# The last down products of a two-layer encoder: halves in another order, an output that already holds its bias, one token tile written transposed

## The chip, the cores and the metric

The kernel runs on one core of one Trainium2 chip. The metric is the device time of one execution in microseconds (us). Before the change, three timed runs gave 1536.09, 1539.66 and 1539.62 us, so the median is 1539.62 us.

## The reference

The program is an encoder trunk of two layers over one sequence of 512 tokens with 1024 channels, all in float32. Each layer has an attention mixer with gated branches, a layer norm, a squared-ReLU MLP with a gated per-layer embedding, and a second layer norm. The change touches the very start (the first input projection) and the very end, which computes the last lines of this (shortened):

```
for i in range(DEPTH):                       # DEPTH = 2
    h = mixer(x)                             # starts with x @ w_in
    x = layer_norm(ALPHA * x + h, ln1_g[i], ln1_b[i])
    mlp = square(relu(x @ w_up[i])) @ w_down[i]
    gate = sigmoid(x @ w_ple_gate[i] + b_ple_gate[i])
    ple = gate * (p[i] @ w_ple[i])
    x = layer_norm(ALPHA * x + mlp + ple, ln2_g[i], ln2_b[i])

layer_norm(x, g, b) = (x - mean) * rsqrt(var + 1e-5) * g + b     # over the 1024 channels of a token
```

## The kernel before

**Precision.** Every large product is made of three TensorE products in the type fp32r: each operand is split into a high part and a low remainder, and high·high, high·low and low·high are summed in PSUM. ScalarE makes the high part by a cast, VectorE the low part by a subtraction (`split`, lines 228 and 229).

**The start.** The residual x comes transposed, as eight tiles `xs` of 128 channels by 512 tokens (line 343), through a pool of four buffers, so that the fifth load waits until the first tile has been split. The weights come in sets of 128 x 1024 (`fetch`, line 249, issued on the queue of SyncE; `prep` splits them). `weights` (called with a look-ahead of two sets) fetches and splits the sets that come next. Only set 0 is asked for between the loads of x, right after the first of them; it comes in three cuts. Sets 1 and 2 are asked for when the first product starts, in program order behind all eight loads of x. The first projection, `linear_k_outer` with the name "start", takes sets 0 to 3, of which set j holds the channels of x tiles 2j and 2j+1. Four output tiles of 128 x 512 are summed side by side, so each set gives 24 products. Here the order of the engines' instructions is set by a planner, which simulates a timeline.

**The MLP.** The hidden layer of 4096 is made in four quarters (`q`). Each quarter's contribution to the output is a product of a 512 x 1024 hidden block with a 1024 x 1024 block of `w_down`, made by seven products of half blocks instead of eight (class `Down`; sums and differences of weight blocks by `add`, of hidden blocks by `hidden`). The seven are in the tuple `PRODUCTS`. Product n has two halves s = 0 and 1, each of which makes a 128 x 512 block in 12 matmuls; below, 4/0 is the half s = 0 of product 4. The output is four token tiles y[0] to y[3] of 128 x 1024. `gather` adds or subtracts a half to its place in y by one VectorE instruction (line 1037). For s = 0 these are y[0] upper columns for product 4, y[2] upper for product 5, y[2] lower for product 6. For s = 1 they are y[1] and y[3] in the same way. Product 3 goes to three places of y (`spread`, line 1028). Products 5 and 6 use one PSUM bank per half: 6 is summed on top of 5, after 5 has been gathered.

**The second norm.** Class `Tokens` computes it: `moments` (line 861) takes the moments of 512 columns, and `statistics` aggregates them (line 868), negates the mean, adds epsilon, takes the reciprocal, lets ScalarE take the root (line 873), subtracts the mean from the whole tile on ScalarE (line 875), and refines the root on VectorE (lines 877 to 879). `scaled` multiplies by the root and by the row g2 (line 896). In the last layer the bias row is added by an accumulating DMA from HBM into y (`add_row`, line 924) for tiles 0 and 1, and by VectorE or GpSimd from a row in SBUF (b2r) for tiles 2 and 3.

**The order at the end.** In the last quarter the products 4, 5 and 6 run with both halves of one before the next: 4/0, 4/1, 5/0, 5/1, 6/0, 6/1. The orders of TensorE, VectorE and ScalarE there are those in which the program is written (`manual_schedule`); those of GpSimd and of the DMA queue of SyncE are the planner's. Tiles 0 and 1 have all their columns after product 4, but they share one `statistics` call. Tiles 2 and 3 each end with a half of product 6. Six DMAs write the output.

Of the kernel before, what the change touches and what calls it, by code (L numbers as in the profile page):

```python
# [10 lines left out]
F32 = mybir.dt.float32  # L11
# [3 lines left out]
ALU = mybir.AluOpType  # L15
# [5 lines left out]
P = 128  # L21
# [180 lines left out]
def build(nc, tc, plan, down, xT, xN, pT, wst, vec, rows, sink, cst, out):  # L202
# [3 lines left out]
    with ctx:  # L206
# [20 lines left out]
        def split(hi, lo, src):  # L227
            nc.scalar.copy(hi, src)  # L228
            nc.vector.tensor_tensor(lo, src, hi.bitcast(F32), ALU.subtract)  # L229
# [110 lines left out]
        with tc.tile_pool(name="xp", bufs=4) as xp:  # L340
            for k in range(KT):
                xs = xp.tile([P, S], F32, tag="xs", name=f"xs{k}")
                nc.sync.dma_start(xs, xT[:, k, :])
                if k == 0:
                    ahead(0)
                split(X[k][0], X[k][1], xs)

# [503 lines left out]
        class Tokens:  # L851
# [5 lines left out]
            def moments(self, a, h):  # L857
                if self.st is None:
                    self.st = self.pool.tile([P, 4, 2, 6], F32, tag="nst", name="nst" + self.name, bufs=1)
                    self.mv = self.pool.tile([P, 4, 2], F32, tag="nmv", name="nmv" + self.name, bufs=1)  # L860
                nc.vector.bn_stats(self.st[:, a, h], self.y[a][:, h * 512:(h + 1) * 512])

            def statistics(self, a, n=2, root=False):
# [3 lines left out]
                for i in range(a, a + n):  # L867
                    nc.vector.bn_aggr(self.mv[:, i], self.st[:, i].rearrange("p h c -> p (h c)"))
                nc.vector.tensor_scalar(m, self.mv[:, a:a + n, 0], -1.0, None, ALU.mult)
# [4 lines left out]
                for i in range(n):  # L874
                    nc.scalar.activation(self.y[a + i], self.y[a + i], AF.Identity, bias=m[:, i:i + 1])
                if root:
# [14 lines left out]
                for i in range(n):  # L891
                    self.rs[a + i] = r[:, i:i + 1]

            def scaled(self, a, g, c=slice(0, D)):
                x = self.y[a][:, c]
                nc.vector.scalar_tensor_tensor(x, x, self.rs[a], g[:, c], ALU.mult, ALU.mult)
# [30 lines left out]
        class Down:  # L927
# [76 lines left out]
            def product(self, q, n, then=None):  # L1004
                name, _, tag, first = self.PRODUCTS[n]
                hi, lo = self.op[name]
                if first:
                    self.bank = getattr(self, "bank", {})
                    self.bank[tag] = [bank(tag, f"dn{self.l}_{q}_{n}_{s}") for s in range(2)]
                ps = self.bank[tag]  # L1010
                for s in range(2):
                    tok = slice(s * P, (s + 1) * P)
                    for c in range(2):
                        w = self.sets[n, c]
                        for i in range(2):
                            k, cols = 2 * c + i, slice(i * 512, (i + 1) * 512)
                            for m, (a, b) in enumerate(((hi, 0), (hi, 1), (lo, 0))):
                                nc.tensor.matmul(ps[s], a[:, k, tok], w[b][:, cols], start=first and not (k or m),  # L1018
                                                 stop=k == 3 and m == 2, skip_group_check=True)
                    last = self.gather(q, n, s, ps[s])  # L1020
                    if then:
                        with tc.issue_after(last.ins):
                            then(s)

# [6 lines left out]
            def gather(self, q, n, s, ps):  # L1031
                y, v, lo, up = self.y, self.v[s], slice(0, 512), slice(512, D)
# [4 lines left out]
                return nc.vector.tensor_tensor(to, to, ps, ALU.subtract if n in (2, 4, 5) else ALU.add)  # L1037
# [21 lines left out]
        for l in range(DEPTH):  # L1059
            last = l == DEPTH - 1  # L1060
            vraw = cp.tile([P, 32], F32, tag="vraw", name=f"vraw{l}", bufs=2)
# [4 lines left out]
            b1, b2 = vraw[:, 16:24], vraw[:, 24:32]  # L1066
# [129 lines left out]
            with tc.manual_schedule(engines={PE}):  # L1196
                for q in range(FQ):
# [58 lines left out]
            with tc.manual_schedule(engines={PE, DVE, ACT}):  # L1256
                dn.cut(q, 6, 0)
                dn.product(q, 4, lambda s: tn.moments(s, 1))
                if last:
                    tn.statistics(0, root=True)  # L1260
                else:
                    ahead(at[0], at[0] + 2)

                def fifth(s):
                    tn.moments(2 + s, 1)
                    if last:
                        if s:
                            tn.scaled(0, g2)
                        return
                    if not s:  # L1270
                        tn.statistics(0)
                        return
                    ahead(at[0] + 1)
                    tn.scaled(0, g2)
                    tn.scaled(1, g2)

                dn.product(q, 5, fifth)
                if last:
                    half = [slice(h * 512, (h + 1) * 512) for h in range(2)]
                    nc.scalar.activation(y[1], y[1], AF.Copy, scale=tn.rs[1])  # L1280
                    for c in half:
                        nc.gpsimd.tensor_tensor(y[1][:, c], y[1][:, c], g2[:, c], ALU.mult)
# [4 lines left out]
                    def sixth(s):  # L1287
                        tn.moments(2 + s, 0)
                        tn.statistics(2 + s, 1, root=True)
                        if not s:  # L1290
                            for c in half:
                                nc.gpsimd.tensor_tensor(y[2][:, c], y[2][:, c], g2[:, c], ALU.mult)

                    dn.product(q, 6, sixth)
                    tn.scaled(3, g2, half[1])
                    nc.gpsimd.tensor_tensor(y[3][:, half[1]], y[3][:, half[1]], b2r[:, half[1]], ALU.add)
                    for c in half:
                        nc.vector.scalar_tensor_tensor(y[2][:, c], y[2][:, c], tn.rs[2], b2r[:, c], ALU.mult, ALU.add)
                        nc.sync.dma_start(out[2][:, c], y[2][:, c])
                    nc.scalar.dma_start(out[3][:, half[1]], y[3][:, half[1]])  # L1300
                    tn.scaled(3, g2, half[0])
                    nc.vector.tensor_tensor(y[3][:, half[0]], y[3][:, half[0]], b2r[:, half[0]], ALU.add)
                    nc.sync.dma_start(out[3][:, half[0]], y[3][:, half[0]])
                else:
# [61 lines left out]
```

## Time and profile before

| | |
|---|---|
| profiled execution, its own time | 1536.4 us |
| its span | 1534.6 us |
| granted TensorE clock | 0.997 |
| TensorE busy | 1512.5 us (99%) |
| VectorE busy | 1017.7 us (66%) |
| ScalarE busy | 763.7 us (50%) |
| GpSimd busy | 246.4 us (16%) |
| DMA | 189.47 MB, mean 123 GB/s |

The span is the time from the first to the last record of the execution; its own time lies 1.8 us above it. PE is TensorE, DVE VectorE, ACT ScalarE, POOL GpSimd and SP SyncE; ACTq, SPq and POOLq are the engines' issuing sides, which start DMAs. A row of the timeline gives the start in us, the duration in us, the engine, the line, the operation, what it writes and reads, and how many instructions of one kind were merged (x2). In brackets stands how long the engine had been idle and what released it.

### The profile page before, as it was taken

The numbers are of one execution on the slowest core, as the hardware profiler recorded it, in microseconds if no ns is written. First come the engines' busy times: TensorE is split into PE (matmuls) and PEld (weight loads), VectorE is DVE, ScalarE is ACT, GpSimd is POOL, SyncE is SP. The second block draws the span as 40 slices with busy tenths as digits, with TensorE's granted clock in tenths as the row PEclk, the third lists the DMA queues.
The fourth block names the chain that finished last, engine by engine and source line by source line (L and its number), as shares of the span: only waits on it lengthen the run. The fifth ranks groups of instructions, "written<-read, shape, count | busy, mean of one in ns | idle before, by whom it ended". The sixth has DMA issues, their size and how long they took to land.

```text
span 1534.6 us, 19685 instructions
## 1 busy us (share of the span) xinstructions
PE 1512.5 (99%) x7438; PEld 1243.0 (81%) x7438; DVE 1017.7 (66%) x1751; ACT 763.7 (50%) x1244; POOL 246.4 (16%) x213
## 2 busy tenths in 40 slices
PE   9999999999999999999999999999999999999996
PEld 7778888888888888888887888878888888888885
DVE  5666553558568777686876665534585776767868
ACT  5777764344344443444557776633442444444442
POOL 1212220110011120202012112111100201111022
PEclk9999999999999999999999999999999999999998
DMA  7544665345612414141355445574455233231403
GB/s 234 124 112 111 149 151 166 123 137 152 205 55 87 133 54 153 42 161 59 100 168 137 114 112 138 138 209 134 149 149 183 69 109 111 82 124 56 151 1 96
DMA packets 53951, 189.47 MB, mean 123 GB/s; under 512 B 6496, under 2 KB 6880, under 8 KB 53856
## 3 DMA queue, kind: packets, MB, share of 16 engines
q1 hardware_dynamic: 43200, 151.74, 30.0%
q0 software_dynamic: 9936, 36.18, 12.5%
q8 instruction: 58, 0.95, 0.3%
q10 hardware_dynamic: 720, 0.30, 0.1%
q14 instruction: 37, 0.30, 0.1%
HBM read 155.16 MB, written 4.19 MB: 104 GB/s over the span
## 4 chain that ended last, share of the span: by engine, by line
PE 88%; DVE 5%; DMA 3%; ACT 2%; issue 1%; POOL 0%; SPq 0%; POOLq 0%; DVEq 0%; ACTq 0%
PE dn L1018 16%; PE ps_up L281 8%; PE ps_up L280 8%; PE ps_up L282 8%; PE pg L288 2%; PE wo L288 2%; PE wo L287 2%; PE wo L286 2%; PE pg L286 2%; PE pg L287 2%; PE sa L439 1%; PE pta L417 1%; DMA raw<-wst 1%; PE sb L439 1%; PE ps_start L281 1%
## 5 line engine op out<-in xcount | busy, mean ns | idle before, releaser
L228 ACT CAST whi<-wst 128x1024 fp32r<-128x1024 f32 (+2 forms) x120 | 121.2, 1010 | 257.8 <-PE ps_up L281 115.5
L229 DVE TENSOR_TENSOR wlo<-wst,whi 128x1024 fp32r<-128x1024 f32 (+2 forms) x120 | 145.5, 1216 | 128.2 <-ACT whi L228 127.4
L280 PE MATMUL ps_up<-xhi,whi 128*128 128x512 f32 x512 | 199.2, 389 | 0.0
L281 PE MATMUL ps_up<-xlo,whi 128*128 128x512 f32 x512 | 199.2, 389 | 0.0
L282 PE MATMUL ps_up<-xhi,wlo 128*128 128x512 f32 x512 | 199.2, 389 | 0.0
L991 POOL TENSOR_TENSOR hr<-r 128x512 f32<-128x512 f32 x64 | 102.2, 1597 | 552.2 <-ACT r L983 531.7
L280 PEld LDWEIGHTS ps_up<-xhi,whi 128*128 128x128 f32 x512 | 96.1, 188 | 20.0
L282 PEld LDWEIGHTS ps_up<-xhi,wlo 128*128 128x128 f32 x512 | 96.1, 188 | 19.9
L281 PEld LDWEIGHTS ps_up<-xlo,whi 128*128 128x128 f32 x512 | 96.1, 188 | 19.9
L228 ACT CAST whi<-raw 128x1024 fp32r<-128x1024 f32 x56 | 58.0, 1053 | 97.0 <-PE ps_up L281 57.7
L228 ACT CAST dhi<-raw 128x1024 fp32r<-128x1024 f32 x56 | 58.7, 1052 | 82.2 <-PE dn L1018 60.1
L1037 DVE TENSOR_TENSOR y<-y,dn 128x512 f32<-128x512 f32 x96 | 65.0, 681 | 38.7 <-PE dn L1018 38.7
L235 POOL DMA_DIRECT2D wlo<-wst x54 | 47.4, 877 | 244.8 <-ACT wlo L234 157.6
L971 DVE TENSOR_TENSOR raw<-raw,raw 128x1024 f32<-128x1024 f32 x64 | 86.3, 1348 | 0.2
L233 ACT CAST whi<-wst 128x1024 fp32r<-128x1024 f32 x54 | 56.7, 1051 | 42.5 <-PE ps_start L281 6.9
L229 DVE TENSOR_TENSOR wlo<-raw,whi 128x1024 fp32r<-128x1024 f32 x56 | 68.1, 1219 | 14.1 <-ACT whi L228 14.1
L229 DVE TENSOR_TENSOR dlo<-raw,dhi 128x1024 fp32r<-128x1024 f32 x56 | 69.2, 1238 | 5.8 <-ACT dhi L228 5.8
L234 ACT ACTIVATE wlo<-whi 128x1024 fp32r<-128x1024 f32 x54 | 57.3, 1061 | 0.9
L288 PE MATMUL pg<-bhi,xlo 128*128 128x512 f32 x128 | 49.9, 390 | 1.2 <-DVE xlo L915 1.2
L1018 PE MATMUL dn<-whi,smh 128*128 128x512 f32 x128 | 50.1, 394 | 0.7 <-DVE y L1037 0.7
L1018 PE MATMUL dn<-wlo,smh 128*128 128x512 f32 x128 | 50.6, 395 | 0.1
L1018 PE MATMUL dn<-whi,sml 128*128 128x512 f32 x128 | 49.9, 390 | 0.0
(846 smaller groups left out, 4014.0 us busy)
## 6 DMA issues: line engine op xcount, KB each, us to landing
wst<-wst SPq DMA_DIRECT2D x187, 512.0 KB, 3.5
raw<-wst SPq DMA_DIRECT2D x64, 512.0 KB, 4.2
wlo<-wst POOLq DMA_DIRECT2D x54, 512.0 KB, 4.6
y<-rows POOLq DMA_DIRECT2D x14, 512.0 KB, 7.2
row<-rows SPq DMA_DIRECT2D x7, 512.0 KB, 8.8
wst<-wst SPq DMA_DIRECT2D x9, 256.0 KB, 2.7
xs<-xT SPq DMA_DIRECT2D x8, 256.0 KB, 6.0
y<-xN SPq DMA_DIRECT2D x4, 512.0 KB, 5.7
```

The source lines that it names most:

```text
L228: nc.scalar.copy(hi, src)
L229: nc.vector.tensor_tensor(lo, src, hi.bitcast(F32), ALU.subtract)
L280: nc.tensor.matmul(ps, w[0][:, s], x[0], start=start, stop=False, skip_group_check=part)
L281: nc.tensor.matmul(ps, w[0][:, s], x[1], start=False, stop=False, skip_group_check=part)
L282: nc.tensor.matmul(ps, w[1][:, s], x[0], start=False, stop=stop, skip_group_check=part)
L286: nc.tensor.matmul(ps, x[0], w[0][:, c], start=start, stop=False)
L287: nc.tensor.matmul(ps, x[0], w[1][:, c], start=False, stop=False)
L288: nc.tensor.matmul(ps, x[1], w[0][:, c], start=False, stop=stop)
L971: nc.vector.tensor_tensor(to, to, other, ALU.add)
L991: nc.gpsimd.tensor_tensor(h.rearrange("p s t -> p (s t)"), r, r, ALU.mult)
L1018: nc.tensor.matmul(ps[s], a[:, k, tok], w[b][:, cols], start=first and not (k or m), stop=k == 3 and m == 2, skip_group_check=True)
L1037: return nc.vector.tensor_tensor(to, to, ps, ALU.subtract if n in (2, 4, 5) else ALU.add)
```

## The change

At the start, x's pool has eight buffers, and set 1 is fetched and split right after x's tile 1. At the end of the last layer the halves run in the order 4/0, 5/0, 4/1, 6/0, and then 5/1 and 6/1 in two pieces of 256 columns each (second pieces in another PSUM bank). The cut of product 5's first weight set moves one half earlier. Each tile has its own statistics, split in two (`in_two`): the first part up to the root, the second with the refinement; between them stands the gather and the moments of another half. Tiles 0, 1 and 2 are no longer centred by themselves: ScalarE applies scale and shift in one instruction per 512 columns. Tiles 0 and 1 are multiplied by g2 on GpSimd and added by an accumulating DMA to the output in HBM, into which the bias row has been written beforehand. Tile 2 is transposed on TensorE, gets g2 and the bias per partition on ScalarE (the vectors `vec` get eight more columns for g2), and is written transposed; the host puts it back. Tile 3 gets (y - mean) * g2 on VectorE (`weighed`), the second half of it after the refinement, and then times root plus bias, in two halves with a DMA each.

```diff
-        with tc.tile_pool(name="xp", bufs=4) as xp:
+        with tc.tile_pool(name="xp", bufs=8) as xp:
...
                 split(X[k][0], X[k][1], xs)
+                if k == 1:
+                    ahead(1)
...
-            def statistics(self, a, n=2, root=False):
+            def steps(self, a, n=2, root=False, centre=True):
...
-                nc.vector.tensor_scalar(m, self.mv[:, a:a + n, 0], -1.0, None, ALU.mult)
+                if centre:
+                    nc.vector.tensor_scalar(m, self.mv[:, a:a + n, 0], -1.0, None, ALU.mult)
                 nc.vector.tensor_scalar(v, self.mv[:, a:a + n, 1], LN_EPS, None, ALU.add)
                 if root:
                     nc.vector.reciprocal(c, v)
                     nc.scalar.activation(rs, c, AF.Sqrt)
-                for i in range(n):
+                for i in range(n if centre else 0):
                     nc.scalar.activation(self.y[a + i], self.y[a + i], AF.Identity, bias=m[:, i:i + 1])
+                if centre is None:
+                    self.weighed(a, 0)
+                yield
...
+                if centre is None:
+                    self.weighed(a, 1)
+                elif not centre:
+                    nc.vector.scalar_tensor_tensor(h, self.mv[:, a:a + n, 0], -1.0, r, ALU.mult, ALU.mult)
+                    for i in range(n):
+                        for y in (self.y[a + i][:, :512], self.y[a + i][:, 512:]):
+                            nc.scalar.activation(y, y, AF.Identity, bias=h[:, i:i + 1], scale=self.rs[a + i])
...
+            def weighed(self, a, h):
+                c = slice(h * 512, (h + 1) * 512)
+                nc.vector.scalar_tensor_tensor(self.y[a][:, c], self.y[a][:, c], self.mv[:, a, 0:1], self.g[:, c],
+                                               ALU.subtract, ALU.mult)
...
+            def half(self, q, n, s, c0=0, c1=512):
...
+                if c0:
+                    self.bank[tag, s] = self.bank.get((tag, s)) or bank("mm", f"dn{self.l}_{q}_{n}_{s}_{c0}")
+                ps = (self.bank[tag, s] if c0 else self.bank[tag][s])[:, c0:c1]
...
-                                if s:
+                                if s != (last and q == FQ - 1 and n == 3):
                                     dn.cut(q, n + 2, 0)
...
+                    with tc.issue_after(dn.ready.ins):
+                        for a in range(2):
+                            nc.sync.dma_start(out[a], rows[l, 4].partition_broadcast(P))
...
+                    def taken(n, s, *cols):
+                        dn.gather(q, n, s, dn.half(q, n, s, *cols), *cols)
+
+                    def weighed(a):
+                        for c in (slice(0, 512), slice(512, D)):
+                            nc.gpsimd.tensor_tensor(y[a][:, c], y[a][:, c], g2[:, c], ALU.mult)
+                        nc.gpsimd.dma_start(out[a], y[a], accum_op=ALU.add)
...
+                    def turned_out(a, h, tag):
+                        tp = bank(tag, f"out{a}_{h}")
+                        ks = range(4 * h, 4 * h + 4)
+                        for i, k in enumerate(ks):
+                            nc.tensor.transpose(tp[:, i * P:(i + 1) * P], y[a][:, k * P:(k + 1) * P], ident)
+                        for i, k in enumerate(ks):
+                            nc.scalar.activation(z[:, k], tp[:, i * P:(i + 1) * P], AF.Identity, bias=b2[:, k:k + 1],
+                                                 scale=gc[:, k:k + 1])
+                        to = out[a].rearrange("(p k) (j t) -> p (k j) t", k=1, j=KT)
+                        nc.sync.dma_start(to[:, ks.start:ks.stop], z[:, ks.start:ks.stop])
+
+                    def roots(a):
+                        return tn.in_two(a, 1, root=True, centre=False)
+
+                    taken(4, 0)
+                    tn.moments(0, 1)
+                    rest = roots(0)
+                    taken(5, 0)
+                    tn.moments(2, 1)
+                    rest()
+                    weighed(0)
+                    taken(4, 1)
+                    tn.moments(1, 1)
+                    rest = roots(1)
+                    taken(6, 0)
+                    tn.moments(2, 0)
+                    rest()
+                    weighed(1)
+                    for n, h in ((5, 2), (6, 0)):
+                        for i in range(2):
+                            taken(n, 1, i * 256, i * 256 + 256)
+                            tn.moments(3, h + i, 4)
+                            if h + i == 2:
+                                rest = roots(2)
+                            if h + i == 3:
+                                rest()
+                    rest = tn.in_two(3, 1, root=True, centre=None)
+                    rest()
+                    for h, tag in enumerate(("pt", "o")):
+                        turned_out(2, h, tag)
+                    for h, issue in enumerate((nc.sync, nc.scalar)):
+                        c = slice(h * 512, (h + 1) * 512)
+                        nc.vector.scalar_tensor_tensor(y[3][:, c], y[3][:, c], tn.rs[3], b2r[:, c], ALU.mult, ALU.add)
+                        issue.dma_start(out[3][:, c], y[3][:, c])
...
-                    for a in range(2):
-                        add_row(y[a], l, 4)
-                        nc.sync.dma_start(out[a], y[a])
...
-                    dn.product(q, 6, sixth)
-                    tn.scaled(3, g2, half[1])
-                    nc.gpsimd.tensor_tensor(y[3][:, half[1]], y[3][:, half[1]], b2r[:, half[1]], ALU.add)
-                    for c in half:
-                        nc.vector.scalar_tensor_tensor(y[2][:, c], y[2][:, c], tn.rs[2], b2r[:, c], ALU.mult, ALU.add)
-                        nc.sync.dma_start(out[2][:, c], y[2][:, c])
-                    nc.scalar.dma_start(out[3][:, half[1]], y[3][:, half[1]])
-                    tn.scaled(3, g2, half[0])
-                    nc.vector.tensor_tensor(y[3][:, half[0]], y[3][:, half[0]], b2r[:, half[0]], ALU.add)
-                    nc.sync.dma_start(out[3][:, half[0]], y[3][:, half[0]])
```

More of the change, by code (lines that the diff above doesn't have):

```diff
@@ L1004, in product @@
             def product(self, q, n, then=None):
[L1005 to L1010, printed above, removed]
-                for s in range(2):
[L1012 to L1020, printed above, removed]
+                for s in range(2):
+                    last = self.gather(q, n, s, self.half(q, n, s))
                     if then:
@@ L1261, in build @@
+                    rest()
[5 more added lines that the diff above has]
+                        issue.dma_start(out[3][:, c], y[3][:, c])
                 else:
+                    dn.product(q, 4, lambda s: tn.moments(s, 1))
@@ L1262, in build @@
                     ahead(at[0], at[0] + 2)
[L1264 to L1277, printed above, removed]
@@ L1305, in build, with fifth @@
+                    def fifth(s):
+                        tn.moments(2 + s, 1)
+                        if not s:
+                            tn.statistics(0)
+                            return
+                        ahead(at[0] + 1)
+                        tn.scaled(0, g2)
+                        tn.scaled(1, g2)
+                    dn.product(q, 5, fifth)
                     PL = [(ph[:, k], pl[:, k]) for k in range(2)]
@@ L1364 @@
     r = run_bass_kernel_spmd(nc, [arrays], core_ids=[0])
-    return np.asarray(r.results[0]["out"]).reshape(1, S, D)
+    o = np.array(r.results[0]["out"])
+    o[2] = o[2].reshape(P, KT, P).transpose(2, 1, 0).reshape(P, D)
+    return o.reshape(1, S, D)
```

60 lines of the change are left out of this document (35 added, 25 removed).

## The prediction

> **What bounds the kernel now.** I read the page first, then the chain of waits, the stretches, and the timelines of the first 30 and the last 55 us.
>
> ```profile
> PE 88%; DVE 5%; DMA 3%; ACT 2%; issue 1%; POOL 0%; SPq 0%; POOLq 0%; DVEq 0%; ACTq 0%
> ```
>
> TensorE holds 88% of the chain, so an edit pays where PE is idle: at the first products and behind the last one. Both are what the change touches. The stretches up to the last matmul and behind it:
>
> ```profile
> 1505.00:1521.10 16.10, 16.10 (x72) 13.01 (x70) 14.60 (x29) 4.70 (x7) 4.57 (x4) 1.00 0.00 1
> 1521.10:1534.60 13.50, 0.02 (x1) 0.00 (x0) 7.82 (x17) 2.33 (x4) 4.89 (x4) 0.61 0.82 233
> ```
>
> Columns: length, then busy time and count of PE, PE's loads, DVE, ACT and POOL, the clock, the DMA share, GB/s. In the first PE is full, DVE nearly, and the DMA engines idle. Then 13.5 us run after PE's end, with DVE busy for 7.8 of them. The end in VectorE's timeline:
>
> ```profile
> 1509.51 0.68 DVE L1037 TENSOR_TENSOR y<-y,dn 128x512 f32<-128x512 f32 x1
> 1510.22 0.69 DVE L861 BATCH_NORM_STATS2 nstn<-y 128x6 f32<-128x512 f32 x1
> 1510.83 0.67 DVE L1037 TENSOR_TENSOR y<-y,dn 128x512 f32<-128x512 f32 x1
> ...
> 1519.53 0.69 DVE L861 BATCH_NORM_STATS2 nstn<-y 128x6 f32<-128x512 f32 x1
> 1520.26 0.21 DVE L868 BATCH_NORM_AGGREGATE nmvn<-nstn 128x2 f32<-128x12 f32 x1
> 1520.50 0.15 DVE L869 TENSOR_SCALAR nsmn<-nmvn 128x1 f32<-128x1 f32 x1
> 1520.58 0.14 DVE L870 TENSOR_SCALAR nsmn<-nmvn 128x1 f32<-128x1 f32 x1
> 1520.75 0.16 DVE L872 RECIPROCAL nsmn<-nsmn 128x1 f32<-128x1 f32 x1
> 1521.18 0.16 DVE L877 TENSOR_TENSOR nsmn<-nsmn 128x1 f32<-128x1 f32 x1 [0.27 <-ACT nsmn L873]
> 1521.38 0.16 DVE L878 SCALAR_TENSOR_TENSOR nsmn<-nsmn 128x1 f32<-128x1 f32 x1
> 1521.57 0.16 DVE L879 SCALAR_TENSOR_TENSOR nsmn<-nsmn 128x1 f32<-128x1 f32 x1
> 1521.65 0.68 DVE L1037 TENSOR_TENSOR y<-y,dn 128x512 f32<-128x512 f32 x1
> ...
> 1524.08 0.70 DVE L877 TENSOR_TENSOR nsmn<-nsmn 128x1 f32<-128x1 f32 x1 [0.33 <-ACT nsmn L873]
> ...
> 1525.28 0.75 DVE L896 SCALAR_TENSOR_TENSOR y<-y,nsmn,row 128x512 f32<-128x512 f32 x1
> 1525.95 2.41 DVE L1298 SCALAR_TENSOR_TENSOR y<-y,nsmn,row 128x512 f32<-128x512 f32 x2
> ...
> 1529.06 0.69 DVE L1302 TENSOR_TENSOR y<-y,row 128x512 f32<-128x512 f32 x1
> ```
>
> DVE has a backlog already at 1509.51, when it gathers 4/0. It works until 1529.75, and the last DMA follows:
>
> ```profile
> 1519.99 1.81 POOL L924 DMA_DIRECT2D y<-rows  x2
> 1522.28 2.48 POOL L1292 TENSOR_TENSOR y<-y,row 128x512 f32<-128x512 f32 x2 [0.47 <-ACT y L875]
> 1526.11 1.70 POOL L1296 TENSOR_TENSOR y<-y,row 128x512 f32<-128x512 f32 x1 [1.35 <-DVE y L896]
> ...
> 1527.85 0.35 ACTq L1300 DMA_DIRECT2D out<-y  x1
> ...
> 1528.46 1.63 SPq L1299 DMA_DIRECT2D out<-y  x2
> 1530.19 0.72 SPq L1303 DMA_DIRECT2D out<-y  x1
> ```
>
> The last issue comes 0.44 us after DVE is done, behind a pair that occupies SP for 1.63. From it to the end of the span are 4.4 us (1534.6 - 1530.19).
>
> **The start.** PE waits twice (timelines of SP, ACT and PE):
>
> ```profile
> 2.60 2.79 SPq L343 DMA_DIRECT2D xs<-xT  x4
> 5.43 1.10 SPq L249 DMA_DIRECT2D wst<-wst  x2
> ...
> 7.72 0.62 ACT L228 CAST whi<-wst 128x512 fp32r<-128x512 f32 x1 [2.00 <-DMA wst<-wst]
> 8.46 2.59 ACT L228 CAST xhi<-xs 128x512 fp32r<-128x512 f32 x4
> 11.69 1.05 ACT L228 CAST whi<-wst 128x1024 fp32r<-128x1024 f32 x1 [0.65 <-DMA wst<-wst]
> 12.96 1.06 ACT L228 CAST whi<-wst 128x1024 fp32r<-128x1024 f32 x1 [0.22 <-DMA wst<-wst]
> ...
> 9.13 1.20 PE L280 MATMUL ps_start<-xhi,whi 128*128 128x512 f32 x4 [1.01 <-ACT xhi L228]
> 12.79 0.50 PE L280 MATMUL ps_start<-xhi,whi 128*128 128x512 f32 x1 [0.65 <-ACT whi L228]
> ```
>
> The second wait, 0.65 us, is for set 1, issued at 5.43 behind x's tiles 1 to 4 and landed at 11.69, 6.3 later. With eight buffers and the earlier call it stands right behind x's tile 1 and is issued at about 3.0. With the same flight it lands at 9.3 and its cast is done by 10.4, while PE needs it at 12.1. So 0.65 goes, with 1.8 to spare. The 1.01 ahead of it stays: it hangs on set 0's last cut (7.72) and the cast behind it on ACT, and what SP issues up to tile 1 is unchanged. Next in line are set 2 and x's later tiles: eight tiles of x and two sets now queue without pause, but set 2 was cast by 14.0 before and is wanted at 17.6 (12.1 and 24 matmuls of 0.227, below). Bounds: 0 if the transfers share the engines so that set 1 lands as late as now, -1.66 if the first wait goes too, and +0.6 if the greater crowd delays set 0's cut by as long as the gain. I take -0.65. Everything behind it follows PE, which is full, so I let it through to the end.
>
> **The end, on PE.** A half is 12 matmuls; 256 columns have been run before, in layer 1's first projection:
>
> ```profile
> 770.08 0.28 PE L281 MATMUL ps_start<-xlo,whi 128*128 128x256 f32 x1
> 770.20 0.28 PE L282 MATMUL ps_start<-xhi,wlo 128*128 128x256 f32 x1
> ...
> 1515.29 0.39 PE L1018 MATMUL dn<-dhi,sml 128*128 128x512 f32 x1
> 1515.52 0.39 PE L1018 MATMUL dn<-whi,axh 128*128 128x512 f32 x1
> ```
>
> From start to start 0.12 against 0.227. A half costs 2.72, two pieces 2.88, so the pieces add 0.32 in all, and PE ends at 1521.4 instead of 1521.1. In the new order 4/0 starts where it did, at 1504.6 (1515.52, where product 6 begins, less four halves); 6/0 ends at 1515.7, and the pieces follow every 1.44. Product 5's first set is now needed at 1507.4 instead of 1510.1; its cut moves ahead of product 3's second `spread`, which leaves 1.5 us. 6/1's pieces wait for the gathers of 5/1's, which below come 0.2 to 0.4 ahead.
>
> **The end, on DVE.** Prices from start to start, in the rows above. Gather to its moments 0.71, moments to the next gather 0.61: a half 1.32. First part of the statistics: aggregate 0.24, epsilon 0.17, reciprocal 0.08, plus 0.12 because the aggregate waits for the moments (0.73 against 0.61): 0.62, and the negated mean is gone. Second part: 0.20, 0.19, 0.08, plus 0.20 for the new shift: 0.67. The 0.43 from reciprocal to refinement, in which ACT makes the root, is now filled by another half. A piece's gather and moments have no row of their own. The nearest is this:
>
> ```profile
> 1487.02 0.42 DVE L999 SCALAR_TENSOR_TENSOR sr<-sr,hr 128x256 f32<-128x256 f32 x1
> ```
>
> 0.42 instead of 0.68, so I take 1.32 - 2 x 0.26 = 0.80 a piece (bounds 0.66, half a half, and 1.32; by the latter the end is 1.5 later). From 1509.51, unchanged because the same casts and spreads stand ahead of it: four halves 5.28, three first parts 1.86, three second parts 2.01, four pieces 3.20, and 0.4 of waiting for PE. That gives 1522.25. For tile 3: first part, without the 0.08, 0.53; a half of `weighed` 0.75, in which the root is made; refinement 0.47; then 0.67 for the other half, 0.67 and 0.75 for the two output instructions. 3.84, so 1526.1. Before it was 1529.75.
>
> **What GpSimd adds.** It now multiplies tile 1 in two instructions of 1.24 each (2.48 x2) from about 1518.5, and tile 2's refinement falls at 1519.8, between them. At 1524.08 the same tiny multiply took 0.70 instead of 0.16 and ended at 1524.78, when POOL's pair ended. Such a wait costs between 0 and one POOL instruction, 1.24. As four dependent steps stand there, one will likely be caught: I take 1.0, and 1527.1. (The Trainium skill's page "SBUF — State Buffer", section "Who interferes with whom", says that a DVE instruction with two SBUF inputs and a GpSimd one that reads SBUF block each other wholly, by order of issue. The 2.41 of the L1298 pair beside a POOL multiply of 1.70 instead of 1.24 agrees; by the page the cost would be the full 1.24 or nothing.) For tile 3 POOL only issues a DMA, and 1521.18 stands beside such an issue at 0.16.
>
> **Off that path.** The bias rows written to the output (two DMAs of 512 KB) go out from about 1490, and have until 1518; the DMA share of 1505 to 1521.1 is 0.00. ACT has six scalings of half a tile, four roots and eight 128x128 copies out of the transposes; the last copies come after tile 3's root at 1523.8 and end by about 1526.5, at bounds of 0.25 and 0.39 each: just ahead of its issue of tile 3's second DMA at 1527.1. If not, 0.5 is late. Tile 2's transposes start after PE's last piece. SP issues tile 2's two DMAs and one of tile 3.
>
> **The sum.** DVE ends 2.65 earlier. The last issue, on ACT's free queue, follows at 0.04 (1527.81 to 1527.85) instead of 0.44: 0.4. The 4.4 behind it stay. The end gives -3.05 (-1.5 with dear pieces, -4.1 without contention), the start -0.65: -3.7 against 1536.4, hence 1532.7. The median shown lies 3.2 above this execution; the runs fall at 1536.1 to 1536.4 or at 1539.6, so the same sum on the median gives 1535.9. I predict between the two, 1534.2.
>
> **The rivals.**
>
> A. *Only the end or only half of it.* Pieces at the price of halves, the full block by GpSimd at both refinements, or set 1 landing no earlier: -1.5 to -2.5, so 1537.5 on the median. For it: DVE has no slack in the new order. Against: each needs the far bound.
>
> B. *The accumulating DMA of tile 1 ends last.* It is issued at about 1521.1 (1518.5 + 2 x 1.24, and the semaphore).
>
> ```profile
> L924 POOL DMA_DIRECT2D y<-rows x14: 862/892/1231, 375.1 to 1520.6; - x14
> DMA to landing us min/median/max: 4.9/7.2/11.3
> ```
>
> At 7.2 it lands at 1528.3, under tile 3's 1531; at 11.3 it sets the end at 1532.4 plus some tenths. That takes back 1.2: -2.5, 1537.1.
>
> C. *The same DMA is far slower because its destination is in HBM, and the kernel gets slower.* No row shows such a one: each packet must read, add and write in the output. It decides from 10 us of flight. At 13.5 the tail is as long as now, and from 19 the whole is over 0.3% slower, 1544. For it: only that accumulates into SBUF already moved slowly. Against: two of them took 7 us together here, and the longest of 14 was 11.3.
>
> D. *More than reckoned.* No contention and both waits of the start gone: -5.8, 1533.8 on the median, 1530.6 on the lower level.
>
> **Chances and range.** Forecast 0.54, A 0.18, B 0.09, C 0.07, D 0.12. About 0.3%, 4.6 us, is what a measurement of this kernel tells from no change. D is beyond it; the forecast's 3.7 is just short, and passes it on the runs that fall on the lower level, or with a little less contention, which I count as two in three; most of C is slower. So faster 0.48 (0.36 and D), slower 0.06, same 0.46. The range runs from D on the lower level to the median less 0.6, where A and most of B lie: 1530 to 1539.
>
> **What would show it.** Right: in the start no wait of PE at set 1; matmuls of 256 columns 0.12 apart; DVE without a wait for ACT's root at tiles 0 to 2; DVE's last instruction near 1526.5 and ACTq's DMA right behind it; accumulating DMAs landed by 1529. Wrong: PE waiting for gathers between the pieces, a wait of the refinement for GpSimd at both tiles, or a span that ends with an accumulating DMA.

## The result, and the profile after

The changed kernel takes 1558.51 us (median; 1556.53 to 1559.95), the kernel before on the same chip 1539.64. The ratio is 1.0127, with a 95% interval of 1.0112 to 1.0142: it is slower by some 19 us, where 1534.2 was forecast, in a range up to 1539. The profiled execution has a span of 1554.8 us (before: 1534.6) at a clock of 0.998.

The two places that I had costed, the end and the start, lose nothing like that. The loss is in between. First the page: total busy times, and the three costliest groups of TensorE with one that did not change (columns of a group: total busy us, mean ns of one instruction, idle time before them). Of after:

```profile
PE 1539.7 (99%) x7470; PEld 1246.7 (80%) x7470; DVE 1017.1 (65%) x1758; ACT 765.8 (49%) x1254; POOL 242.4 (16%) x212
...
L282 PE MATMUL ps_up<-xhi,wlo 128*128 128x512 f32 x512 | 202.0, 395 | 0.0
L280 PE MATMUL ps_up<-xhi,whi 128*128 128x512 f32 x512 | 202.0, 395 | 0.0
L281 PE MATMUL ps_up<-xlo,whi 128*128 128x512 f32 x512 | 202.0, 395 | 0.0
```

Of before:

```profile
L280 PE MATMUL ps_up<-xhi,whi 128*128 128x512 f32 x512 | 199.2, 389 | 0.0
```

PE is busy for 27.2 us more (1539.7 against 1512.5). Each of the three groups of the up projection grew by 2.8 us, with the same count, form and line, and no idle time: 6 ns (395 against 389) on every matmul of 512 columns. The edit touches none of these lines. Not every group grew. From the view that groups by line and form, of after (the same three rows of before are at 389 or 390 ns; the first of them is shown behind):

```profile
L286 PE MATMUL wo<-bhi,ahm 128*128 128x512 f32 x64 | 25.2, 394 | 0.0
L286 PE MATMUL wo<-whi,ahm 128*128 128x512 f32 x64 | 24.9, 389 | 0.0
L286 PE MATMUL pg<-bhi,xhi 128*128 128x512 f32 x128 | 49.9, 390 | 0.0
```

Of before:

```profile
L286 PE MATMUL wo<-bhi,ahm 128*128 128x512 f32 x64 | 24.9, 389 | 0.0
```

The line, the shapes and the types of the three rows of after are alike; they differ in which tiles they read. So the next thing to look at is where those tiles lie.

**Where the tiles lie.** The edit widens the tile of the vectors, of which there are two:

```diff
-            vraw = cp.tile([P, 32], F32, tag="vraw", name=f"vraw{l}", bufs=2)
+            vraw = cp.tile([P, 40], F32, tag="vraw", name=f"vraw{l}", bufs=2)
```

Eight columns of 4 bytes in two tiles are 64 bytes per partition. Everything that the allocator places behind them moves on by 64 bytes. From the addresses of the two built programs (bytes within a partition):

```
tile            before   after
xhi  (x)          1664    1664    ahead of vraw, did not move
vraw, second     34560   34592
whi  (weights)   47232   47296    moved by 64
ahm  (hidden)    88192   88256    moved by 64
```

Before, whi and xhi were 45568 = 178 x 256 bytes apart; after, 64 more than such a multiple. That sorts the three rows: in `pg<-bhi,xhi` neither operand moved (390), in `wo<-whi,ahm` both did (389), in `wo<-bhi,ahm` one did (394). To test it on all matmuls I took from the trace the time from the start of each 512-column matmul to the start of the next, and from the program two start addresses: that of the operand that streams, and that of the operand loaded for the next matmul (with the operand loaded for the same matmul the groups come out nearly the same; the runs don't tell the two apart). The difference of the two, modulo 512 bytes, with the mean time:

```
difference   before              after
0            227.4 ns (x5615)    227.1 ns (x673)
448          231.8 ns (x18)      233.3 ns (x3631)
64           -                   230.2 ns (x1294)
other        230.0 ns (x74)      230-233 ns (x92)
```

In the program 126 matmuls are at a difference other than 0 before, and 5200 after (3758 at 448, 1316 at 64, 126 others). The 92 in the row "other" of after stand ahead of narrower matmuls, as those at 448 and "other" do before; they show nothing of the addresses. At their excess over 227.4 ns the two large groups cost 3758 x 5.9 + 1316 x 2.8 ns = 25.9 us, close to the growth of PE's busy time (27.2). It is so far a correlation; the first experiments below test it.

**The end after.** The last two stretches, columns as in the prediction:

```profile
1527.80:1544.00 16.20, 16.20 (x94) 14.19 (x93) 15.10 (x37) 5.12 (x9) 5.34 (x5) 1.00 0.13 20
1544.00:1554.80 10.80, 2.06 (x15) 1.37 (x13) 6.13 (x17) 4.52 (x11) 1.57 (x2) 0.70 0.68 167
```

The last product ends at 1544.74, so the span ends 10.06 us behind it; before it was 13.5. VectorE's timeline from the gather of 4/0:

```profile
1532.80 0.68 DVE L1073 TENSOR_TENSOR y<-y,dn 128x512 f32<-128x512 f32 x1
...
1538.59 0.16 DVE L887 RECIPROCAL nsmn<-nsmn 128x1 f32<-128x1 f32 x1
1539.12 0.69 DVE L1073 TENSOR_TENSOR y<-y,dn 128x512 f32<-128x512 f32 x1 [0.37 <-PE dn L1057]
...
1541.10 0.41 DVE L1073 TENSOR_TENSOR y<-y,dn 128x256 f32<-128x256 f32 x1
1541.55 0.43 DVE L865 BATCH_NORM_STATS2 nstn<-y 128x6 f32<-128x256 f32 x1
1541.89 0.19 DVE L882 BATCH_NORM_AGGREGATE nmvn<-nstn 128x2 f32<-128x12 f32 x1
...
1543.17 0.27 DVE L895 TENSOR_TENSOR nsmn<-nsmn 128x1 f32<-128x1 f32 x1
1543.47 1.22 DVE L896 SCALAR_TENSOR_TENSOR nsmn<-nsmn 128x1 f32<-128x1 f32 x1
1544.73 0.16 DVE L897 SCALAR_TENSOR_TENSOR nsmn<-nsmn 128x1 f32<-128x1 f32 x1
...
1546.69 0.26 DVE L882 BATCH_NORM_AGGREGATE nmvn<-nstn 128x2 f32<-128x24 f32 x1
...
1549.03 1.41 DVE L1354 SCALAR_TENSOR_TENSOR y<-y,nsmn,row 128x512 f32<-128x512 f32 x2
```

From 1532.80 to 1550.44 are 17.64 us, where 17.59 were forecast (1509.51 to 1527.1). GpSimd's and ScalarE's timelines, and the transfers of the tile `out`:

```profile
1537.72 2.55 POOL L1307 TENSOR_TENSOR y<-y,row 128x512 f32<-128x512 f32 x2 [29.81 <-ACT y L917]
1540.68 0.91 POOL L1308 DMA_DIRECT2D out<-y  x1 [0.41 <-POOL y L1307]
1542.13 2.55 POOL L1307 TENSOR_TENSOR y<-y,row 128x512 f32<-128x512 f32 x2 [0.53 <-ACT y L917]
1545.08 0.90 POOL L1308 DMA_DIRECT2D out<-y  x1 [0.41 <-POOL y L1307]
```
```profile
1547.55 2.89 ACT L1318 ACTIVATE z<-out,vraw 128x128 f32<-128x128 f32 x8
1550.47 0.37 ACTq L1355 DMA_DIRECT2D out<-y  x1
```
```profile
DMA to landing us min/median/max: 2.2/2.8/5.6
```

The last DMA goes out 0.03 us behind VectorE's last instruction. ScalarE's copies end at 1550.44 too, so nothing was to spare there. And the accumulating DMAs into HBM are at most 5.6 us on their way: the one issued at 1545.08 has landed by 1551.6.

**The start after**, in the timelines of SP, ACT and PE:

```profile
3.07 0.43 SPq L249 DMA_DIRECT2D wst<-wst  x1
4.35 3.24 SPq L343 DMA_DIRECT2D xs<-xT  x6
...
12.04 1.27 SPq L1298 DMA_DIRECT2D out<-rows  x2
```
```profile
4.19 0.62 ACT L228 CAST xhi<-xs 128x512 fp32r<-128x512 f32 x1 [1.25 <-DMA xs<-xT]
...
6.30 0.62 ACT L228 CAST whi<-wst 128x512 fp32r<-128x512 f32 x1 [0.74 <-DMA wst<-wst]
...
9.33 1.05 ACT L228 CAST whi<-wst 128x1024 fp32r<-128x1024 f32 x1 [0.83 <-DMA wst<-wst]
...
16.03 1.05 ACT L228 CAST whi<-wst 128x1024 fp32r<-128x1024 f32 x1 [0.31 <-DMA wst<-wst]
20.12 1.05 ACT L228 CAST whi<-wst 128x1024 fp32r<-128x1024 f32 x1 [3.04 <-DMA wst<-wst]
```
```profile
5.06 0.80 PE L280 MATMUL ps_start<-xhi,whi 128*128 128x512 f32 x1 [0.51 <-ACT whi L228]
...
7.04 0.63 PE L281 MATMUL ps_start<-xlo,whi 128*128 128x512 f32 x1
7.46 0.63 PE L280 MATMUL ps_start<-xhi,whi 128*128 128x512 f32 x1
```

Set 1 is cast at 9.33 (forecast 9.3), and neither of PE's two waits, 1.01 and 0.65 us, is left. But the first products come 0.43 us apart instead of 0.23, and the first instruction behind the projection starts at 29.41 us, 0.17 later than before. The bias rows, which I had put at about 1490, go out at 12.04: the planner placed them among the weights of the start.

### The profile page after: what moved, and what is told of

It is laid out like the page before. It is cut to its first block, busy times and chain, and to the rows that moved or that the text cites. A ratio compares the mean times of both kernels' runs of the same rounds, so it can differ in the third digit from the quotient of the medians.

```text
span 1554.8 us, 19763 instructions
## 1 busy us (share of the span) xinstructions
PE 1539.7 (99%) x7470; PEld 1246.7 (80%) x7470; DVE 1017.1 (65%) x1758; ACT 765.8 (49%) x1254; POOL 242.4 (16%) x212
## 4 chain that ended last, share of the span: by engine, by line
PE 92%; DVE 4%; DMA 2%; ACT 1%; issue 1%; SPq 0%; DVEq 0%; ACTq 0%
PE dn L1057 16%; PE ps_up L282 8%; PE ps_up L281 8%; PE ps_up L280 8%; PE wo L287 2%; PE wo L288 2%; PE wo L286 2%; PE pg L288 2%; PE pg L287 2%; PE pg L286 2%; PE sa L441 1%; PE sb L441 1%; PE pta L419 1%; PE ps_start L280 1%; PE ps_start L281 1%; PE ps_start L282 1%
## 5 line engine op out<-in xcount | busy, mean ns | idle before, releaser
L1073 DVE TENSOR_TENSOR y<-y,dn 128x512 f32<-128x512 f32 (+1 forms) x98 | 65.6, 672 | 43.0 <-PE dn L1057 43.0
L1057 PE MATMUL dn<-wlo,smh 128*128 128x512 f32 (+1 forms) x130 | 51.3, 395 | 0.3
L1057 PE MATMUL dn<-whi,smh 128*128 128x512 f32 (+1 forms) x130 | 50.5, 391 | 0.3
L1057 PE MATMUL dn<-dlo,smh 128*128 128x512 f32 (+1 forms) x130 | 50.6, 389 | 0.0
```

The lines of the kernel that those rows point to most:

```text
L1057: nc.tensor.matmul(ps, a[:, k, tok], w[b][:, cols], start=first and not (k or m), stop=k == 3 and m == 2, skip_group_check=True)
```

## The experiments

Ratios are against the kernel before, run beside each on the same chip. In several kernels the only edit is the width of `wgap` (line 223), a small tile of zeros that nothing but its own memset touches, which lies directly ahead of the weight tiles; each of its columns moves everything behind it by 4 bytes.

**The kernel before, everything behind `wgap` 64 bytes further on.** If the place of the tiles is the cause, this alone must be as slow as the change.

```diff
-        wgap = wp.tile([P, 32], F32, name="wgap", bufs=1)
+        wgap = wp.tile([P, 48], F32, name="wgap", bufs=1)
```

> The kernel before, with a filler tile in front of the weight pool 64 bytes larger per partition and nothing else. Theory P (place): eight more columns of the vectors, twice 32 bytes, moved every weight tile by 64 bytes, and a matmul of 512 columns takes 233 ns instead of 227 when the start addresses of its moving and its stationary operand differ by 64 modulo 128. Then this kernel, which has none of the change's operations, is slower by about 24 us, near 1563, with the up products 233 ns apart. Rival O (operations): the loss comes from what the change does (pieces, bias rows, order); then this one stays at 1539.6 with 227 ns.

Measured: 1561.23 us, ratio 1.0139 (1.0115 to 1.0163); matmuls at the difference 448 took 233.3 ns.

```profile
L280 PE MATMUL ps_up<-xhi,whi 128*128 128x512 f32 x512 | 202.2, 395 | 0.0
```

But for the width of the filler not one instruction differs from before, and the whole loss is there. It is the place, not the new order or its DMAs.

**Which places are good: 128 bytes?** The same edit in the kernel after (48 columns: 128 bytes from before's places), and 64 columns in the kernel before (128 bytes).

> The changed kernel, with the same filler 64 bytes larger, so that the weight tiles start on a line of 128 bytes again. Theory P: the up products are 227 ns apart again and what is left of the change shows, 3 to 4 us less than before, 1535 to 1536.5. Rival O: it stays at 1558.

> The kernel before, with the filler 128 bytes larger. Theory P: the rest modulo 128 is what it was, so 1539.6 within 0.2%. If any move of the tiles costs (another rule than modulo 128, or a planner that answers to addresses), it is slower, by up to the 24 us of the 64-byte move.

Measured: 1557.39 us, 1.0117 (1.0093 to 1.0141), and 1562.11 us, 1.0146 (1.0116 to 1.0176), with 232 to 233 ns at the differences 128 and 384. Theory P, modulo 128, had both back at full pace, and missed: a multiple of 128 is not enough.

**Difference, or the weights' own address?** x and the weights both 64 bytes further on, by a small tile ahead of both:

```diff
         # kernel before, behind ident, ahead of xhi
+        igap = cp.tile([P, 16], F32, name="igap")
+        nc.gpsimd.memset(igap, 0.0)
```

> The kernel before, with 64 bytes put in front of the hidden state's tiles too, so that the moving operand x and the weights both start 64 off. Theory P in its form R (the difference between the two operands counts): the up products stay at 227 ns; only products of one operand from the left and one from the right side of SBUF (down, output and gate products, 800 to 2400 of them) get slower, so plus 5 to 12 us. Form S (the stationary operand must start on a line of 128 bytes) or M (the moving one must): up products at 233 ns and plus 20 us or more.

Measured: 1545.41 us, 1.0037 (1.0023 to 1.0051). The up projection, whose two operands moved together, is back (line numbers are 2 higher in this kernel):

```profile
L282 PE MATMUL ps_up<-xhi,whi 128*128 128x512 f32 x512 | 199.2, 389 | 0.0
```

The weights lie where they lie in the slow kernel, and their matmuls take 389 ns. It is the difference that counts, not the own address of either operand, since both moved. Nor is it the DMAs that fill the moved tiles, since they go to the same places here. What is left of the loss is in products with one operand in a pool that did not move (848 matmuls at 448 took 233.3 ns, 1324 at 64 took 229.0).

**The change, with before's differences restored.** 144 columns of `wgap` in the kernel after: 64 and 448 bytes make 512.

```diff
-        wgap = wp.tile([P, 32], F32, name="wgap", bufs=1)
+        wgap = wp.tile([P, 144], F32, name="wgap", bufs=1)
```

> The changed kernel with the filler in front of the weight pool 448 bytes larger, so that the weights stand a whole multiple of 512 bytes from where they stood before. Theory P512 (a matmul of 512 columns takes 227 ns only where the start addresses of its two operands differ by a multiple of 512 bytes): nearly all products return to 227 ns, and what is left is the change itself: 3.0 to 4.5 us faster than before, near 1536. Rival O (the change's own operations cost): stays above 1550.

Measured: 1535.42 us, 0.9978 (0.9967 to 0.9988), with 5576 matmuls at the difference 0 and 227.4 ns. The change itself gains 3.4 us (1.8 to 5.1). Against the kernel after, the 448 bytes are worth 23.1 us.

**256 or 512?** 96 columns in the kernel before: 256 bytes further on.

> The kernel before with the filler 256 bytes larger. Theory P512: still 5100 products at a difference of 256 modulo 512, 229 to 234 ns, so slower by 15 to 25 us, 1555 to 1565. Form P256 (256 bytes are the unit): unchanged, 1540.

Measured: 1539.01 us, 1.0000 (0.9989 to 1.0010); 4937 matmuls at the difference 256 took 227.4 ns. A whole 256 bytes costs nothing; the 512 of theory P512 was too much.

**The end alone and the start alone.** The end: the kernel after with 144 columns of `wgap`, its start as before. The start: the kernel before with the new start.

```diff
         # the end alone, against the kernel after (beside wgap)
-        with tc.tile_pool(name="xp", bufs=8) as xp:
+        with tc.tile_pool(name="xp", bufs=4) as xp:
...
-                if k == 1:
-                    ahead(1)
```

> As the changed kernel with 448 bytes more in the filler, but with the start of before (four buffers for x, set 1 fetched where it was). The step on the end: DVE's chain and the free queue give 3 us; 1536.5 to 1537.5. With the run that has both, the difference is the start's share: 0.65 by the forecast, nothing if the later first load takes back what the earlier second set gives.

> The kernel before with nothing but the start of the change (eight buffers for x, set 1 fetched behind x's tile 1). No tile of the weights moves. By the forecast 0.65 us faster, 1539; by the profile of the changed kernel, where x's first tile was split 0.5 us later than before and PE waited 0.5 us for it, between 0 and 0.6 faster, not to be told from no change.

Measured: the end alone 1537.64 us, 0.9992 (0.9981 to 1.0002); the start alone 1538.82 us, 0.9994 (0.9984 to 1.0003). Neither is told from no change by itself: -1.2 us (-2.9 to +0.3) and -0.9 (-2.5 to +0.5). They sum to -2.1, within the interval of both together. The 3.05 forecast for the end lies just outside its interval. By the difference between the kernel with both and the end alone the start would be worth 2.2; by its own run it is worth 0.9. So the times don't settle the shares. In the trace of the start alone the projection ends 1.78 us earlier than before.

I don't read the end's worth from whole spans of single profiles. Ahead of the products `ya`, near 1035 us of the kernel before, PE waits 2.7 to 4.5 us for ScalarE in the profiles of ten of the eleven experiments, with and without the change, but 1.9 us in that of before, which was a low run (1536.4 against a median of 1539.6). Of before, and of the kernel with 96 columns:

```profile
L280 PE MATMUL ya<-oah,whi 128*128 128x512 f32 x64 | 25.6, 401 | 1.9 <-ACT gate L847 1.9
```
```profile
L280 PE MATMUL ya<-oah,whi 128*128 128x512 f32 x64 | 26.4, 413 | 4.5 <-ACT gate L847 4.5
```

The time behind PE's last product varies little: 13.5 to 13.6 us with the old end (before, 96 columns, start alone), and 9.7 to 9.8 in the four kernels that have the new end and before's differences (the end alone, the change with 144 columns, and the two that follow).

**Without the wider tile, and the bias rows late.** In the first kernel `vraw` goes back to 32 columns and the g2 columns get a tile of their own, which puts the weights at before's places without a filler. In the second, beside that, ScalarE issues the bias rows in the last stage.

```diff
         # both, against the kernel after
-            vraw = cp.tile([P, 40], F32, tag="vraw", name=f"vraw{l}", bufs=2)
-            nc.scalar.dma_start(vraw, vec[l])
+            vraw = cp.tile([P, 32], F32, tag="vraw", name=f"vraw{l}", bufs=2)
+            nc.scalar.dma_start(vraw, vec[l][:, 0:32])
...
+                    gc = qp.tile([P, KT], F32, name="gc", bufs=1)
+                    nc.sync.dma_start(gc, vec[l][:, 32:40])
         # the second alone
-                    with tc.issue_after(dn.ready.ins):
-                        for a in range(2):
-                            nc.sync.dma_start(out[a], rows[l, 4].partition_broadcast(P))
+                    for a in range(2):
+                        nc.scalar.dma_start(out[a], rows[l, 4].partition_broadcast(P))
```

> The kernel after, with the vectors' tile back at 32 columns (the eight columns of g2 come as a tile of their own in the last stage), so that the weight tiles lie where the kernel before has them, without a filler. Theory P (the price of a 512-column matmul goes by the difference of its two start addresses, in units of 256 B): as the kernel after with the filler that restored the difference (1535.42), so 1534.5 to 1535.5; the matmuls at 227 ns. Theory V (the wider load of the vectors delays x's first tile): beside this, the first cast of x begins at 3.6 to 3.9 us instead of 4.1 to 4.4, the first products of PE come 0.23 us apart instead of 0.43, and the start ends 0.5 to 1 us sooner. Rival C (the fetch of set 1 that goes out among x's cuts delays it, whatever the width of the vectors): the first cast again at 4.1 to 4.4 and the products 0.43 us apart; 1535.5 to 1536.5.

> As the run before it (vectors at 32 columns), and the two DMAs that put the bias rows into the output go out from ScalarE in the last stage instead of from SyncE where the planner puts them (at 12 us, among the weights of the start). If they cost the start something there: 0.3 to 0.8 us less than the run before it, with the fourth set's cast at 16.7 us instead of 20. If they cost nothing there, as PE did not wait for that set: the same time within 0.3 us. Either way the end stays as it is in the kernel after, about 10 us behind PE's last matmul.

Measured: 1533.76 us, 0.9968 (0.9953 to 0.9982), and 1533.54 us, 0.9968 (0.9956 to 0.9980). Both beat the kernel before by 4.9 us; they are the fastest here, not told apart from each other, nor, with overlapping intervals, from the 448-byte filler's 0.9978. So the early bias rows cost nothing that can be measured. Nor do they make a set late, as one of the expectations had it; that compared different sets. The casts of sets 1 to 4 start at 11.69, 12.96, 16.73 and 20.13 before, and at 9.33, 14.67, 16.03 and 20.12 after. Set 3, the last of the start's four, is not late; the cast at 20.12 is that of set 4, the first of the next stage. With the rows late it starts at 19.86. Of before and of the kernel with the rows late:

```profile
16.73 1.05 ACT L228 CAST whi<-wst 128x1024 fp32r<-128x1024 f32 x1 [2.71 <-DMA wst<-wst]
```
```profile
19.86 1.05 ACT L228 CAST whi<-wst 128x1024 fp32r<-128x1024 f32 x1 [2.82 <-DMA wst<-wst]
```

The slow first products were the other question. In the first of the two kernels x's first tile is cast at 4.07 although the vectors are narrow, and PE is at full pace. That goes against both theories: the one on the width of the vectors said 3.6 to 3.9, the one on the crowd said products 0.43 apart. The stretch from 4.5 to 9 us (PE's busy time and count first) of before, of that kernel, and of the kernel before with the weights 32 bytes further on (next experiment):

```profile
4.50:9.00 4.50, 3.60 (x13) 2.34 (x12) 2.00 (x5) 1.68 (x4) 0.00 (x0) 1.00 0.99 326
```
```profile
4.50:9.00 4.50, 4.09 (x16) 2.84 (x16) 2.91 (x6) 2.27 (x6) 0.00 (x0) 1.00 0.96 289
```
```profile
4.50:9.00 4.50, 4.35 (x10) 2.93 (x10) 2.20 (x6) 1.87 (x5) 0.00 (x0) 1.00 0.96 315
```

In the third the old start, with x's first tile cast at 3.71 and PE hardly idle, gets only 10 products into 4.35 us of busy time. So neither a late first tile nor PE's idling goes with the slow pace. Across the thirteen profiles it lasts to about 9 us in three, for a few products in two, and for at most one or two in the rest. The granted clock in these rows is 1.00 throughout, so the rows don't show the cause.

The Trainium skill's page "TensorE: Matmul & The Clock Gate", section "What's actually happening", says that the array runs at half clock until it has been seen busy, and that the watching window runs free, so that the number of slow matmuls differs between runs of one kernel. A pace of 0.43 against 0.23 and a length that differs between the profiles agree with it; no run here shows the gate itself.

**How small a shift hurts.** 40 columns of `wgap` in the kernel before: 32 bytes.

> The kernel before with the weight tiles 32 B further on, so that the differences of the two start addresses are 32 and 480 modulo 512. Theory P (a mismatch of any size below 256 B costs the same): 227 ns becomes 230 to 233 ns, 1558 to 1564. Rival F (the unit of transfer is 32 B or 64 B wide and only a shift of a full 64 B matters): 1539, matmuls at 227 ns. Rival H (the loss grows with the distance from a multiple of 256 B): between, about 1550, 229 to 230 ns.

Measured: 1565.72 us, 1.0174 (1.0157 to 1.0192).

```profile
L280 PE MATMUL ps_up<-xhi,whi 128*128 128x512 f32 x512 | 202.5, 396 | 0.0
```

233.3 ns at both differences, 480 and 32 (64 had cost 230.2). The shift of 32 bytes, the smallest tried, costs no less than the larger ones (its ratio is the highest, with an interval that overlaps theirs); so the loss does not shrink with the distance from a multiple of 256. The time is even 1.7 us above the expected range.

## Why the prediction was wrong, and where it was right

**The step that failed** stands at the end of the paragraph on the start: "Everything behind it follows PE, which is full, so I let it through to the end." That PE is full was right (99% busy in both). Behind it stood, unsaid, that each matmul keeps its price. I had taken 0.227 us as the price of a 512-column matmul and used it in the kernel after, though in these kernels it holds only while the start addresses of the two operands differ by a multiple of 256 bytes. The eight columns more in the tile of the vectors, which I costed at nothing, moved the weights by 64 bytes against x, and 5200 of the matmuls went to 230 to 233 ns. The term missing from the sum is +23 us (the kernel after against the same with before's differences; 21 by the filler alone). None of the rivals held it: A and B end at 1537.5 and 1537.1, and C, the one on the slow side, put the loss at the accumulating DMA. The first experiment shows the missing term without the change, the fifth the change without the term.

**The rest of the sum held as a whole.** Forecast -3.7; with the differences restored, -3.4 (-5.1 to -1.8), and -4.9 (-7.2 to -2.8) with the narrow tile. How it splits between the end and the start is seen in the traces alone. By its terms:

- The end: forecast 3.05 earlier, with PE itself 0.3 later, so some 3.4 off the time behind PE. The trace of after shows 3.44 off (13.5 to 10.06), those of the four kernels with before's differences 3.7 to 3.8. The timed run of the end alone (-1.2, at most -2.9) does not confirm it.
- VectorE's chain: 17.59 forecast, 17.64 measured. A piece was put at 0.80; the first takes 0.79 (1541.10 to 1541.89). The wait for PE was put at 0.4; it is 0.37.
- GpSimd's block: I took 1.0 of 0 to 1.24. At tile 2's refinement the operations of 0.14 and 0.16 took 0.27 and 1.22, which ends at 1544.69, when GpSimd's pair ends (1544.68): 1.19 in all. Tile 1's refinement, at 1540.46, falls behind the other pair, and is free.
- Rivals B and C: refuted. The longest flight of a DMA of that tile was 5.6 us, not 10 or more, and the span ends 4.3 us behind the last plain DMA's issue.
- The bias rows: my time for them (1490) was wrong by the whole kernel. The planner, not the place in the text, sets SP's order, as I had noted of the kernel before. It happened to cost nothing.
- The start: set 1 landed as forecast, and the wait of 0.65 is gone. The other wait, of 1.01, which I had said would stay, shrank (0.33 and 0.76 us in two profiles) or went. In the four kernels with the new start in which PE soon found its pace, the projection ends 1.3 to 1.8 us earlier than in before (29.24), more than the 0.65 that I took and about the -1.66 that I gave as a bound; against the earliest of the other profiles with the old start (28.89) it is 1.0 to 1.5. In the profile of after, and in that of the one with 144 columns of `wgap` and both parts, the first products are slow and the projection ends later than before (+0.17 and +0.27). The bound of +0.6 for set 0's cut was not needed: the cut was cast at 6.30, earlier than before (7.72; 6.98 in the kernel with 96 columns).

**Open.** Why a difference of the addresses costs TensorE time: I know how large the price is and from which difference on, not which part of the memory or of the engine collides. Why PE's first products run slow in some profiles. And the shares of the start and the end in the gain, neither of which the timing tells from nothing; the traces put the end above what its own run allows.

## What to carry to other kernels

Before the price of an instruction is carried from the old profile to the new kernel, see whether its operands still lie at the same addresses: a tile widened by a few bytes moves everything allocated behind it, and where PE is full, 3 to 6 ns on 5000 matmuls outweigh the 3 to 5 us of an edit at the ends. If every matmul of one form changes by the same one or two per cent though its line was not touched, compare the addresses first. For 512-column fp32r matmuls like these, keep the start addresses of streamed and loaded operands a multiple of 256 bytes apart. A new small tile is better placed behind the operands than added to a tile ahead of them, as the kernel with the g2 columns in a tile of their own shows.

## What the runs showed of the hardware

- A 512-column fp32r matmul started every 227 ns when the start addresses of the streaming and the loaded operand differed by 0 or 256 modulo 512 bytes, and every 229 to 233.3 ns at the six other differences tried on many (32, 64, 128, 384, 448, 480). With some 5200 such matmuls the kernels took 1.2 to 1.7% longer than the kernel before.
- Matmuls of 256 columns show no such price: 118 ns at the difference 448 (some 95 in the kernel after), 120 at 0 in the kernel before (medians).
- Two accumulating DMAs of 512 KB each into HBM landed within 5.6 us (profile of after).
- PE's first products after its warm-up ran 0.43 us apart for up to 4 us in some profiles, at a granted clock of 1.00 in the rows.
